# Raw weights in blocks of 512 columns, and operand buffers taken in turn, in a two-layer diffusion backbone

## The chip, the cores and the metric

The kernel runs on one core of one Trainium2 chip, as one program. The metric is the time of one execution in device microseconds; the time before is the median of three runs. Engines are named as in the profile: PE is TensorE's matrix multiplication, PEld its weight load, DVE is VectorE, ACT is ScalarE, POOL is GpSimd, SP is SyncE, which here only issues transfers.

## The reference

Two layers run over 512 latent tokens and 256 context tokens of 1024 features. Layer 0 mixes tokens with windowed attention, layer 1 with a gated linear recurrence in both directions. Each layer ends with a gated feed-forward with a convolution of three tokens. Every sub-layer is preceded by a norm and a shift and scale computed from two conditioning vectors. All is float32. Cut down:

```python
for layer in range(2):
    mod   = silu(c)     @ ada_w[layer] + ada_b[layer]     # 6 x 1024: shift, scale, gate, twice
    mod_c = silu(c_ctx) @ ada_w[layer] + ada_b[layer]
    hx = rms_norm(x, norm1_g) * (1 + sc1) + sh1           # hc the same for ctx
    yx, yc = windowed_gqa(hx, hc, attn_w_in, attn_w_out, ...) if layer == 0 else \
             hgrn2_bidir(hx, hc, hgrn_w_in, hgrn_w_out, ...)
    x = x + g1 * yx
    hx2 = rms_norm(x, norm2_g) * (1 + sc2) + sh2
    gate, val = split(hx2 @ w_up)                         # w_up: 1024 x 2*2816
    x = x + g2 * ((silu(dwconv3(gate)) * val) @ w_down)   # w_down: 2816 x 1024
    # layer 0: ctx goes through the same steps
return x
```

## The kernel before, in words

Activations lie with features on partitions, in 8 groups of 128. Every product of two float32 matrices is done as three TensorE products of a reduced format: each operand is held as a high part and the rest. For a weight, ScalarE copies the raw float32 columns into `wh` and VectorE writes the difference into `wl`; this pair of instructions is called the split here. A pair (`wh`, `wl`) of 512 columns is an operand, and its buffers come from `operand()` (L84), which asks the pools in the list `wsp` one after the other and rotates the list. `ws0` has four buffers of each kind, `wsC`, `wsD` and `wsE`, which are added after the attention, after the first feed-forward and before the second, have two each.

Raw weights land in the pool `wp`: two buffers of 2048 columns (8 KB in each partition). `load_raw` (L90) takes one buffer for all parts of a load, one transfer for each part. Three callers share `wp`:

- `load_w` (L99), for all projections and the second feed-forward's w_up. With `cols` it reads w_down in a transfer of 256 output columns for `nf` feature groups and splits each half through a strided view.
- `load_pair` (L125), for w_up in the first feed-forward, where gate and value are computed by a scheme of seven products for a 2 by 2 block matrix (Strassen's), so sums of the four quarters of the buffer are made on VectorE, partly in place, and seven operands are split from them (L140, L141).
- `ada_steps` (L301), the conditioning: a step loads 128 rows by 2048 columns of `ada_w` in one transfer of 1 MB and multiplies it as it is, in four matmuls side by side in the array's columns (L309). Five groups of eight such steps are strewn over the attention and the first feed-forward; the first group's columns are loaded on their own at the start (`ar`, L296).

The stages are: first norm and projections of keys and values (to about 75 us), attention with the query projections in between (to about 345 us), `attn_out` (L870 on), the first feed-forward (`ffn`, from about 443 us), the recurrence (`hgrn`, from about 1004 us), its output projection `hgrn_out`, and the second feed-forward (from about 1490 us). A feed-forward runs in rounds: some `up(ft)`, each a feature group of gate and value, then for each of four pairs of output groups (`dp`) a load of w_down and the product `dn`, whose result VectorE adds to x (`xl`, `xc`, L1023). `hn` is the scaled x of the next layer, split in the same way (L362, L363); `hs` (L392) holds the sums of the activations that the seven products need, `y` their inputs.

The order of instructions on each engine is made by the framework's scheduler, which simulates the program with its own time model and takes ready instructions by priority; the splits are given a priority of 180 instructions ahead (`W_AHEAD`). A tile's buffer is given on when its last reader is done. All loads of weights go through SP's queue, in the order the scheduler gives them; a load that waits for its buffer holds those behind it.

Of the kernel before, what the change touches and what calls it, by code (L numbers as in the profile page):

```python
# [8 lines left out]
F32 = mybir.dt.float32  # L9
F32R = mybir.dt.float32r  # L10
BF16 = mybir.dt.bfloat16
AF = mybir.ActivationFunctionType
ALU = mybir.AluOpType
# [3 lines left out]
P = 128  # L17
# [14 lines left out]
W_AHEAD = 180  # L32
# [32 lines left out]
def ap(t, off, *dims):  # L65
    return bass.AP(t.tensor, t.offset + off, [list(t.ap[0])] + [list(d) for d in dims])


def f(t):
    return t.bitcast(F32)  # L70


class Kernel:
# [13 lines left out]
        self.wsp = self.wsp[1:] + self.wsp[:1]  # L87
        return pool.tile([P, 512], F32R, tag="wh", name="wh"), pool.tile([P, 512], F32R, tag="wl", name="wl")

    def load_raw(self, parts):  # L90
        raw = self.wp.tile([P, 2048], F32, tag="wr", name="wr")
        n = 0
        for src in parts:
            nk, m = src.shape[1:]
            self.nc.sync.dma_start(out=raw[:, n:n + nk * m].rearrange("p (k m) -> p k m", m=m), in_=src)
            n += nk * m
        return raw, n

    def load_w(self, parts, cols=False):  # L99


        nc = self.nc
        raw, n = self.load_raw(parts)
        nk, m = parts[0].shape[1:]
        out = []
        for lo in range(0, m, P) if cols else range(0, n, 1024):
            size = nk * P if cols else min(1024, n - lo)
            ops = []
            for i in range(0, size, 512):
                c = min(512, size - i)  # L110
                wh, wl = (t[:, 0:c] for t in self.operand())
                src = raw[:, lo + i:lo + i + c]
                with self.tc.high_priority(offset=W_AHEAD):
                    if cols:
                        src = ap(raw[:, i // P * m + lo:i // P * m + lo + 1], 0, (m, c // P), (1, P))
                        wh, wl = (t.rearrange("p (k c) -> p k c", c=P) for t in (wh, wl))
                    nc.scalar.activation(wh, src, AF.Copy)  # L117
                    nc.vector.tensor_tensor(wl, src, f(wh), op=ALU.subtract)  # L118
                    if cols:
                        wh, wl = (t.rearrange("p k c -> p (k c)") for t in (wh, wl))  # L120
                ops.append((wh, wl))
            out.append(ops)
        return out

    def load_pair(self, parts, tmp):  # L125


        nc = self.nc
        raw, n = self.load_raw(parts)
        q = n // 4  # L130
        a11, a12, a21, a22 = (raw[:, i * q:(i + 1) * q] for i in range(4))
        s1 = tmp.tile([P, 512], F32, tag="s1", name="s1")[:, 0:q]
        ops = [tuple(t[:, 0:q] for t in self.operand()) for _ in range(7)]

        def total(o, x, y, op):
            nc.vector.tensor_tensor(o, x, y, op=op)
            return o

        def parts(i, src):
            nc.scalar.activation(ops[i][0], src, AF.Copy)  # L140
            nc.vector.tensor_tensor(ops[i][1], src, f(ops[i][0]), op=ALU.subtract)  # L141


        with self.tc.high_priority(offset=W_AHEAD):
            parts(0, a11)
            parts(1, a12)
            total(s1, a21, a22, ALU.add)
            s3 = total(a21, a11, a21, ALU.subtract)
            s2 = total(a11, s1, a11, ALU.subtract)
            parts(3, s2)  # L150
            parts(6, s3)
            parts(2, s1)
            parts(5, a22)
            s4 = total(a12, a12, s2, ALU.subtract)
            parts(4, s4)
        return ops

    def wcols(self, w, lo, n):
# [142 lines left out]
    def ada_steps(self, l, r, pool, tag, width):  # L301

        nc = self.nc
        ps = pool.tile([P, width], F32, tag=tag, name="ada")
        for k in range(KT):
            raw = self.wp.tile([P, 2048], F32, tag="wr", name="wada")
            nc.sync.dma_start(out=raw, in_=self.a["ada_w"][l, k * P:(k + 1) * P, r * 2048:(r + 1) * 2048])
            for j in range(4):
                nc.tensor.matmul(ps[32 * j:32 * j + 32, 0:512], lhsT=self.cs[:, k, :], rhs=raw[:, j * 512:(j + 1) * 512],  # L309
                                 start=(k == 0), stop=(k == KT - 1), tile_position=(0, 32 * j))  # L310
            if k < KT - 1:
                yield
        sb = self.ap_.tile([P, 512], F32, tag=self.ap_tag, name="adas")
        nc.vector.tensor_copy(sb, ps[:, 0:512])
        yield
        pt = pool.tile([P, width], F32, tag=tag, name="adat")
        for i in range(4):
            nc.tensor.transpose(pt[:, i * P:(i + 1) * P], sb[:, i * P:(i + 1) * P], self.ident)
        m = self.mod[l]
        for v in range(2):  # L320
            o = ap(m[:, v, r * 16:r * 16 + 1], 0, (1, 4), (4, 4))
            b = ap(self.adab[l][:, r * 16:r * 16 + 1], 0, (1, 4), (4, 4))
            i_ = ap(pt[:, v:v + 1], 0, (P, 4), (32, 4))
            nc.vector.tensor_tensor(o, i_, b, op=ALU.add)
        if r == 0:
            self.gain_scale(l, 0, 8, self.n1g[l])
        if r == 2:
            self.gain_scale(l, 1, 32, self.n2g[l])
        yield
# [628 lines left out]
    def ffn(self, l, hs, R, rows, lat_only, tmp, acp, bk, gp, done, side=None):  # L958
        nc, a = self.nc, self.a
        wup, wdn = a["ffn_w_up"][l], a["ffn_w_down"][l]  # L960
        half = C0 // 2 if lat_only else hs[0].shape[3]
        n = LAT if lat_only else TW
# [36 lines left out]
        f0, late, ahead = 0, None, []  # L999
        for r, nf in enumerate(ROUNDS[l]):  # L1000
            gt = ahead + [up(ft) for ft in range(f0 + len(ahead), f0 + nf)]

            ahead = [up(f0 + nf)] if f0 + nf < NFF else []
            if side and r < 5:
                next(side, None)
            for dp in range(KT // 2):
                w = self.load_w([wdn[f0 * P:(f0 + nf) * P, dp * 256:dp * 256 + 256].rearrange("(k p) m -> p k m", p=P)], True)
                outs = [[(bank("dn")[:, 0:m], c) for _, c, m in segs] for _ in range(2)]

                def down(j, ks):  # L1010
                    for _ in self.mm_steps(w[j], ks, lambda k: (gt[k][:, 0], gt[k][:, 1]), outs[j], ks[0] == 0, ks[-1] == nf - 1):
                        pass


                part = dp == 0 and not ahead
                if part:
                    for j in range(2):
                        down(j, range(nf - 1))
                for j in range(2):
                    d = 2 * dp + j  # L1020
                    down(j, (nf - 1,) if part else range(nf))
                    for v, ((o, _), (_, _, x)) in enumerate(zip(outs[j], self.segs(lat_only))):
                        nc.vector.scalar_tensor_tensor(x[:, d], o, self.modc(l, v, 5, d), x[:, d], op0=ALU.mult, op1=ALU.add)  # L1023
                    if f0 + nf == NFF:
                        if late is not None:
                            done(late, bank)
                        late = d
            f0 += nf
# [273 lines left out]
    def run(self, stop=99):  # L1302
        nc, a = self.nc, self.a
        top = ExitStack()
        self.cp = self.pool(top, "const")
        self.wp = self.pool(top, "wp", 2)
        self.ws0 = self.pool(top, "ws0", 4)
        self.wsp = [self.ws0]
        self.setup()
# [6 lines left out]

        xp = self.pool(top, "xp")
        self.xl = xp.tile([P, KT, LAT], F32, tag="xl", name="xl")
        self.wsp.append(self.pool(top, "wsC", 2))
        Rp = self.pool(top, "Rp", 1)  # L1320
        pjs = ExitStack()
        pj = self.pool(pjs, "pj", 2, PSUM)
# [6 lines left out]
        es = ExitStack()  # L1329
        tmp = self.pool(es, "tmpA", 1)  # L1330
# [40 lines left out]
        pjs.close()  # L1371
        pj = self.pool(pjs, "pj", 2, PSUM)
        es = ExitStack()
        self.wsp.append(self.pool(top, "wsD", 2, right=True))
        e2 = ExitStack()
        sc = self.pool(e2, "sc", 2, PSUM)
        lv = self.pool(e2, "lv", 2, PSUM)
# [14 lines left out]
        es = ExitStack()  # L1392
        tmp = self.pool(es, "tmpB", 2)
        acp = self.pool(es, "accB", 1)
        gp = self.pool(es, "gpB", 9)
        self.wsp.append(self.pool(es, "wsE", 2))
        bk = self.pool(es, "bkB", 8, PSUM)
        rows = self.row_factor(acc, True, tmp, bk, "ps", 512, R, -1.0, (gp, "g"))
        ost = {}
# [53 lines left out]
```

## Time and profile before

| | |
|---|---|
| median of 3 runs | 1877.1 us (1875.34 to 1877.72) |
| the profiled execution | 1872.88 us, its span 1871.1 us |
| mean granted TensorE clock | 0.988 |
| HBM read, written | 162.27 MB, 2.10 MB |
| w_up, `wr` | 88 transfers of 512 KB |
| conditioning, `wada` | 40 transfers of 1024 KB |
| hgrn_w_in, `wr` | 40 transfers of 512 KB |
| w_down, `wr` | 16 of 512 KB, 8 of 896 KB, 8 of 384 KB, 4 of 1024 KB |
| attn_w_in, attn_w_out, hgrn_w_out | 6 of 1024 KB, 8 of 512 KB, 8 of 512 KB |

The span is the time from the first to the last recorded work of one execution, and the times of the other views count from its start. "Busy" for PE includes the modelled end of each pipelined matmul, so two matmuls that follow each other overlap in the record. A wait row tells how long an engine stood idle before an instruction and what released it last.

### The profile page before, as it was taken

The numbers are of one execution on the slowest core, as the hardware profiler recorded it, in microseconds if no ns is written. First come the engines' busy times: TensorE is split into PE (matmuls) and PEld (weight loads), VectorE is DVE, ScalarE is ACT, GpSimd is POOL, SyncE is SP. The second block draws the span as 40 slices with busy tenths as digits, with TensorE's granted clock in tenths as the row PEclk, the third lists the DMA queues.
The fourth block names the chain that finished last, engine by engine and source line by source line (L and its number), as shares of the span: only waits on it lengthen the run. The fifth ranks groups of instructions, "written<-read, shape, count | busy, mean of one in ns | idle before, by whom it ended". The sixth has DMA issues, their size and how long they took to land.

```text
span 1871.1 us, 32302 instructions
## 1 busy us (share of the span) xinstructions
PE 1801.3 (96%) x13326; PEld 1576.9 (84%) x13326; DVE 1214.1 (65%) x2243; ACT 754.7 (40%) x1478; POOL 247.4 (13%) x233
## 2 busy tenths in 40 slices
PE   6999999998999999999998999999998999999998
PEld 4976786787888888989887888988886799899997
DVE  5575667466867686766777676777676655455462
ACT  4354555465534252434354333333332443233332
POOL 1233333103201000101013101111110200000000
PEclk9999999998999999999998999999999999999999
DMA  9204104232333333233313212122220332333321
GB/s 309 66 23 158 47 24 169 68 102 68 124 113 102 113 124 113 91 113 124 113 61 90 58 35 58 35 57 58 57 69 24 90 91 91 90 96 96 92 82 65
DMA packets 204416, 166.44 MB, mean 89 GB/s; under 512 B 5149, under 2 KB 198254, under 8 KB 199150
## 3 DMA queue, kind: packets, MB, share of 16 engines
q1 hardware_dynamic: 196608, 160.47, 27.8%
q10 hardware_dynamic: 7662, 3.92, 0.7%
q8 instruction: 105, 1.72, 0.4%
q14 instruction: 41, 0.34, 0.1%
HBM read 162.27 MB, written 2.10 MB: 88 GB/s over the span
## 4 chain that ended last, share of the span: by engine, by line
PE 87%; DVE 5%; DMA 4%; issue 2%; ACT 1%; POOL 1%; SPq 0%; ACTq 0%; POOLq 0%; DVEq 0%
PE dn L170 15%; PE pd L170 13%; PE pZ L188 8%; PE pf L170 8%; PE pV L188 4%; PE pjq L598 4%; PE pv L170 4%; PE ao L170 4%; PE ho L170 3%; PE pq L170 3%; PE pv L824 2%; PE pt L816 2%; PE ada L309 2%; PE pY L188 2%; PE pgate L170 2%; PE kv L598 2%
## 5 line engine op out<-in xcount | busy, mean ns | idle before, releaser
L117 ACT ACTIVATE wh<-wr 128x512 fp32r<-128x512 f32 (+1 forms) x320 | 193.0, 618 | 452.3 <-DMA wr<-in_ffn_w_up 74.8
L118 DVE TENSOR_TENSOR wl<-wr,wh 128x512 fp32r<-128x512 f32 (+1 forms) x320 | 223.6, 705 | 140.3 <-ACT wh L117 138.3
L170 PE MATMUL dn<-g,wh 128*128 128x512 f32 (+1 forms) x1056 | 263.3, 357 | 2.2 <-ACT g L995 2.2
L170 PE MATMUL pd<-hn,wh 128*128 128x256 f32 (+1 forms) x1408 | 227.3, 284 | 0.9 <-issue 0.9
L170 PEld LDWEIGHTS dn<-g,wh 128*128 128x128 f32 x1056 | 175.4, 189 | 32.7 <-ACT g L995 2.8
L170 PEld LDWEIGHTS pd<-hn,wh 128*128 128x128 f32 x1408 | 194.2, 190 | 2.5 <-issue 2.3
L188 PE MATMUL pZ<-hs,wh 128*128 128x386 f32 x704 | 185.2, 345 | 3.0 <-ACT wh L140 1.5
L170 PE MATMUL dn<-g,wl 128*128 128x512 f32 (+1 forms) x528 | 159.4, 356 | 0.0
L140 ACT ACTIVATE wh<-wr 128x512 fp32r<-128x512 f32 x132 | 81.6, 628 | 167.9 <-DMA wr<-in_ffn_w_up 47.4
L170 PE MATMUL pd<-hn,wl 128*128 128x256 f32 x704 | 141.8, 283 | 0.0
L188 PEld LDWEIGHTS pZ<-hs,wh 128*128 128x128 f32 x704 | 128.0, 190 | 15.7 <-ACT wh L140 4.4
L141 DVE TENSOR_TENSOR wl<-wr,wh 128x512 fp32r<-128x512 f32 x132 | 94.0, 717 | 53.6 <-ACT wh L140 53.5
L170 PE MATMUL pf<-hn,wh 128*128 128x512 f32 (+1 forms) x512 | 119.3, 349 | 9.7 <-DVE xc L1023 8.8
L188 PE MATMUL pZ<-hs,wl 128*128 128x386 f32 x352 | 119.4, 343 | 2.2 <-DVE wl L141 2.2
L926 POOL TENSOR_TENSOR gg<-gg,R 128x772 f32<-128x772 f32 x22 | 53.9, 2449 | 458.3 <-DVE gg L925 446.6
L170 PEld LDWEIGHTS pd<-hn,wl 128*128 128x128 f32 x704 | 109.0, 190 | 0.0
L1023 DVE SCALAR_TENSOR_TENSOR xl<-dn,mod,xl 128x512 f32<-128x512 f32 x72 | 53.9, 748 | 73.7 <-PE dn L170 73.6
L170 PEld LDWEIGHTS dn<-g,wl 128*128 128x128 f32 x528 | 87.4, 188 | 14.8
L170 PEld LDWEIGHTS pf<-hn,wh 128*128 128x128 f32 x512 | 80.9, 192 | 22.5 <-ACT wh L117 9.1
L188 PE MATMUL pV<-hs,wh 128*128 128x386 f32 x352 | 92.2, 341 | 5.0 <-ACT hs L392 5.0
L598 PE MATMUL pjq<-wh,hn 128*128 128x256 f32 x384 | 77.8, 291 | 0.0
L188 PEld LDWEIGHTS pZ<-hs,wl 128*128 128x128 f32 x352 | 66.7, 190 | 6.6 <-DVE gg L925 3.4
(299 smaller groups left out, 3807.1 us busy)
## 6 DMA issues: line engine op xcount, KB each, us to landing
wr<-in_ffn_w_up SPq DMA_DIRECT2D x88, 512.0 KB, 5.1
wada<-in_ada_w SPq DMA_DIRECT2D x40, 1024.0 KB, 4.8
wr<-in_hgrn_w_in SPq DMA_DIRECT2D x40, 512.0 KB, 4.2
ar<-in_ada_w SPq DMA_DIRECT2D x32, 256.0 KB, 7.1
wr<-in_ffn_w_down SPq DMA_DIRECT2D x16, 512.0 KB, 4.1
wr<-in_ffn_w_down SPq DMA_DIRECT2D x8, 896.0 KB, 4.7
wr<-in_attn_w_in SPq DMA_DIRECT2D x6, 1024.0 KB, 8.1
wr<-in_attn_w_out SPq DMA_DIRECT2D x8, 512.0 KB, 4.9
```

The costliest lines, as they stand in the source:

```text
L117: nc.scalar.activation(wh, src, AF.Copy)
L118: nc.vector.tensor_tensor(wl, src, f(wh), op=ALU.subtract)
L140: nc.scalar.activation(ops[i][0], src, AF.Copy)
L141: nc.vector.tensor_tensor(ops[i][1], src, f(ops[i][0]), op=ALU.subtract)
L170: nc.tensor.matmul(o, lhsT=wt, rhs=at[:, t0:t0 + o.shape[1]], start=(first and n == 0 and i == 0), stop=(last and n == len(ks) - 1 and i = ...
L188: self.nc.tensor.matmul(ps, lhsT=wt, rhs=at, start=(first and k == 0 and i == 0), stop=(k == nk - 1 and i == 2), skip_group_check=not first)
L309: nc.tensor.matmul(ps[32 * j:32 * j + 32, 0:512], lhsT=self.cs[:, k, :], rhs=raw[:, j * 512:(j + 1) * 512], start=(k == 0), stop=(k == KT ...
L598: nc.tensor.matmul(out, lhsT=x, rhs=y[:, wk], start=(start and k == 0 and j == 0), stop=(stop and k == KT - 1 and j == 2))
L816: nc.tensor.transpose(pt[:, j * P:(j + 1) * P], pr[j][:, b * P:(b + 1) * P], self.ident)
L824: nc.tensor.matmul(pv[a * HD:(a + 1) * HD, 0:256], lhsT=V[:, tl, g, :], rhs=pT[:, a * 256:(a + 1) * 256], start=(b == 0), stop=(b == len(t ...
L926: times = lambda eng, o, x, y: eng.tensor_tensor(o, x, y, op=ALU.mult)
L1023: nc.vector.scalar_tensor_tensor(x[:, d], o, self.modc(l, v, 5, d), x[:, d], op0=ALU.mult, op1=ALU.add)
```

## The change

`wp` becomes eight buffers of 512 columns, the same memory. `block` takes one buffer for each 512 columns of a load and issues one transfer for it; `split` splits one block. `load_w` cuts every part into blocks; w_down is read by 128 output columns at a time, so no strided view is left. `load_pair` loads its four quarters as four blocks. A conditioning step loads four blocks of 512 columns and then does its four matmuls. The list of operand pools is written out anew at each place where it grew: `ws0`, `wsC`, `ws0` during `attn_out` and the first feed-forward, `ws0`, `wsC`, `ws0`, `wsD` in the recurrence, and `wsE` behind these four in the second feed-forward, where each pool stood once in the list before.

```diff
-    def load_raw(self, parts):
-        raw = self.wp.tile([P, 2048], F32, tag="wr", name="wr")
...
+    def block(self, src, pool=None):
+        nk, m = src.shape[1:]
+        raw = (pool or self.wp).tile([P, 512], F32, tag="wr", name="wr")[:, 0:nk * m]
+        self.nc.sync.dma_start(out=raw.rearrange("p (k m) -> p k m", m=m), in_=src)
+        return raw
+
+    def split(self, src, op=None):
+        wh, wl = op or (t[:, 0:src.shape[1]] for t in self.operand())
+        with self.tc.high_priority(offset=W_AHEAD):
+            self.nc.scalar.activation(wh, src, AF.Copy)
+            self.nc.vector.tensor_tensor(wl, src, f(wh), op=ALU.subtract)
+        return wh, wl
+
+    def load_w(self, parts):
+        out = []
         for src in parts:
             nk, m = src.shape[1:]
+            step = 512 // m
+            blocks = [self.block(src[:, k:min(k + step, nk)]) for k in range(0, nk, step)]
+            ops = [self.split(b) for b in blocks]
+            out += [ops[i:i + 2] for i in range(0, len(ops), 2)]
         return out
...
     def load_pair(self, parts, tmp):
-        raw, n = self.load_raw(parts)
-        q = n // 4
-        a11, a12, a21, a22 = (raw[:, i * q:(i + 1) * q] for i in range(4))
+        a11, a12, a21, a22 = (self.block(p[:, i:i + 4]) for p in parts for i in (0, 4))
...
     def ada_steps(self, l, r, pool, tag, width):
         for k in range(KT):
-            raw = self.wp.tile([P, 2048], F32, tag="wr", name="wada")
-            nc.sync.dma_start(out=raw, in_=self.a["ada_w"][l, k * P:(k + 1) * P, r * 2048:(r + 1) * 2048])
+            raw = []
             for j in range(4):
-                nc.tensor.matmul(..., rhs=raw[:, j * 512:(j + 1) * 512], ...)
+                raw.append(self.wp.tile([P, 512], F32, tag="wr", name="wada"))
+                nc.sync.dma_start(out=raw[j], in_=self.a["ada_w"][l, k * P:(k + 1) * P, r * 2048 + j * 512:r * 2048 + j * 512 + 512])
+            for j in range(4):
+                nc.tensor.matmul(..., rhs=raw[j], ...)
...
-                w = self.load_w([wdn[f0 * P:(f0 + nf) * P, dp * 256:dp * 256 + 256].rearrange("(k p) m -> p k m", p=P)], True)
+                w = self.load_w([wdn[f0 * P:(f0 + nf) * P, d * P:d * P + P].rearrange("(k p) m -> p k m", p=P)
+                                 for d in (2 * dp, 2 * dp + 1)])
...
-        self.wp = self.pool(top, "wp", 2)
+        self.wp = self.pool(top, "wp", 8)
...
-        self.wsp.append(self.pool(top, "wsC", 2))
+        wsC = self.pool(top, "wsC", 2)
+        self.wsp = [self.ws0, wsC, self.ws0]
...
-        self.wsp.append(self.pool(top, "wsD", 2, right=True))
+        wsD = self.pool(top, "wsD", 2, right=True)
+        self.wsp = [self.ws0, wsC, self.ws0, wsD]
...
-        self.wsp.append(self.pool(es, "wsE", 2))
+        self.wsp = [self.ws0, wsC, self.ws0, wsD, self.pool(es, "wsE", 2)]
```

More of the change, by code (lines that the diff above doesn't have):

```diff
@@ L88, in operand @@
         return pool.tile([P, 512], F32R, tag="wh", name="wh"), pool.tile([P, 512], F32R, tag="wl", name="wl")
-    def load_raw(self, parts):
-        raw = self.wp.tile([P, 2048], F32, tag="wr", name="wr")
-        n = 0
+    def block(self, src, pool=None):
[9 more added lines that the diff above has]
+        return wh, wl
@@ L93, in load_raw @@
+    def load_w(self, parts):
+        out = []
         for src in parts:
             nk, m = src.shape[1:]
[L95 to L102, printed above, removed]
-        raw, n = self.load_raw(parts)
[L104 to L122, printed above, removed]
@@ L128, in load_pair @@
         nc = self.nc
-        raw, n = self.load_raw(parts)
-        q = n // 4
-        a11, a12, a21, a22 = (raw[:, i * q:(i + 1) * q] for i in range(4))
-        s1 = tmp.tile([P, 512], F32, tag="s1", name="s1")[:, 0:q]
-        ops = [tuple(t[:, 0:q] for t in self.operand()) for _ in range(7)]
+        a11, a12, a21, a22 = (self.block(p[:, i:i + 4]) for p in parts for i in (0, 4))
+        s1 = tmp.tile([P, 512], F32, tag="s1", name="s1")
+        ops = [self.operand() for _ in range(7)]
         def total(o, x, y, op):
@@ L137, in total @@
             return o
-        def parts(i, src):
-            nc.scalar.activation(ops[i][0], src, AF.Copy)
-            nc.vector.tensor_tensor(ops[i][1], src, f(ops[i][0]), op=ALU.subtract)
         with self.tc.high_priority(offset=W_AHEAD):
-            parts(0, a11)
-            parts(1, a12)
+            self.split(a11, ops[0])
+            self.split(a12, ops[1])
             total(s1, a21, a22, ALU.add)
@@ L149, in load_pair @@
             s2 = total(a11, s1, a11, ALU.subtract)
[L150 to L153, printed above, removed]
+            self.split(s2, ops[3])
+            self.split(s3, ops[6])
+            self.split(s1, ops[2])
+            self.split(a22, ops[5])
             s4 = total(a12, a12, s2, ALU.subtract)
-            parts(4, s4)
+            self.split(s4, ops[4])
         return ops
@@ L305, in ada_steps @@
         for k in range(KT):
-            raw = self.wp.tile([P, 2048], F32, tag="wr", name="wada")
-            nc.sync.dma_start(out=raw, in_=self.a["ada_w"][l, k * P:(k + 1) * P, r * 2048:(r + 1) * 2048])
+            raw = []
             for j in range(4):
-                nc.tensor.matmul(ps[32 * j:32 * j + 32, 0:512], lhsT=self.cs[:, k, :], rhs=raw[:, j * 512:(j + 1) * 512],
+                raw.append(self.wp.tile([P, 512], F32, tag="wr", name="wada"))
+                nc.sync.dma_start(out=raw[j], in_=self.a["ada_w"][l, k * P:(k + 1) * P, r * 2048 + j * 512:r * 2048 + j * 512 + 512])
+            for j in range(4):
+                nc.tensor.matmul(ps[32 * j:32 * j + 32, 0:512], lhsT=self.cs[:, k, :], rhs=raw[j],
                                  start=(k == 0), stop=(k == KT - 1), tile_position=(0, 32 * j))
```

## The prediction

> **What bounds the kernel now.** I read the page first: the engines' shares, the busy tenths, the loads.
>
> ```profile
> span 1871.1 us, 32302 instructions
> PE 1801.3 (96%) x13326; PEld 1576.9 (84%) x13326; DVE 1214.1 (65%) x2243; ACT 754.7 (40%) x1478; POOL 247.4 (13%) x233
> DMA  9204104232333333233313212122220332333321
> q1 hardware_dynamic: 196608, 160.47, 27.8%
> ```
>
> TensorE is busy for 1801.3 of 1871.1 us. The DMA engines are near their limit only in the first slice, and q1 takes 27.8% of them over the span. The change touches no matmul and no activation, so what it can win lies in TensorE's 69.8 idle us (1871.1 - 1801.3). The second view is the list of waits, TensorE's own (engine, line, what it waited for: total us, times, longest):
>
> ```profile
> PE ada L275 <- DMA ar<-in_ada_w: 10.8, 3, 9.0
> PE pf L170 <- DVE xc L1023: 8.8, 1, 8.8
> PE pV L188 <- ACT hs L392: 5.0, 1, 5.0
> PE pZ L188 <- DVE wl L141: 2.2, 3, 1.6
> PE dn L170 <- ACT g L995: 2.2, 2, 1.7
> PE ada L309 <- DMA wada<-in_ada_w: 1.9, 2, 1.6
> PE ao L170 <- ACT wh L117: 1.6, 1, 1.6
> PE pZ L188 <- ACT wh L140: 1.5, 4, 0.4
> PE pY L188 <- ACT wh L140: 0.6, 1, 0.6
> ```
>
> The reader is to see how little of it names a weight: wl 2.2, wh 1.5 and 0.6, wh of attn_out 1.6, wada 1.9, together 7.8 us. The big ones are the first loads (10.8), and the borders between stages (8.8 and 5.0). The stages themselves, in the view by stretches (length, then busy us of TensorE, weight load, VectorE, ScalarE, GpSimd, then the granted clock, DMA share, GB/s):
>
> ```profile
> 0.00:40.00 40.00, 22.15 (x224) 15.13 (x228) 24.71 (x76) 18.25 (x31) 5.98 (x9) 1.00 0.91 302
> 400.00:440.00 40.00, 35.73 (x210) 30.67 (x209) 25.56 (x45) 25.11 (x58) 6.56 (x12) 0.98 0.21 63
> 440.00:480.00 40.00, 36.70 (x186) 32.29 (x186) 32.41 (x49) 19.08 (x38) 13.87 (x14) 0.89 0.25 80
> 960.00:1000.00 40.00, 33.20 (x188) 28.92 (x186) 31.86 (x46) 20.14 (x39) 11.79 (x6) 0.98 0.27 80
> 1520.00:1560.00 40.00, 40.00 (x336) 40.00 (x335) 23.92 (x48) 15.07 (x24) 0.00 (x0) 1.00 0.33 91
> ```
>
> The last feed-forward is full (40.00 of 40.00) and has nothing to give. The borders at 400 to 480 and at 960 to 1000 lose 4.3, 3.3 and 6.8 us.
>
> **The change, part by part.** First the loads become more and smaller. The page's DMA issues (KB each, median us to landing) and SP's waits:
>
> ```profile
> wr<-in_ffn_w_up SPq DMA_DIRECT2D x88, 512.0 KB, 5.1
> wada<-in_ada_w SPq DMA_DIRECT2D x40, 1024.0 KB, 4.8
> xs<-in_x ACTq DMA_DIRECT2D x8, 256.0 KB, 2.7
> SPq L95 <- DVE wl L118: 754.3, 69, 34.9
> L307 SPq DMA_DIRECT2D wada<-in_ada_w x40: 327/340/649, 74.1 to 920.5; - x40
> L95 SPq DMA_DIRECT2D wr<-in_ffn_w_up x88: 367/472/1832, 391.7 to 1778.6; - x88
> ```
>
> A pair of w_up goes from two issues to four and a conditioning step from one to four: 88 to 176 and 40 to 160, so 208 more. Each costs SP 0.34 to 0.47 us (the last two rows, min/median/max in ns), so 71 to 98 us over the span. SP sits 754.3 us in one kind of wait alone, for a raw buffer that the split (wl) still reads; the issues hide there. The other loads grow in the same way, by less, and hide in the same wait. Packets of w_down halve from 256 columns to 128; with the DMA engines at a quarter of their time I cost that at nothing. If that cover went, for instance in the first slice, where the share is 0.91, it would cost: the two tiles of attn_w_in between the ar loads become eight loads, six more issues of up to 0.4 us, at most 2.4 us for the ar loads behind them in SP's queue, on which TensorE's 10.8 us hang. Against it ScalarE gets its first block earlier. I take +0.5, ends -1 and +2.4.
>
> Second, a first block lands sooner. The nearest rows are 5.1 us for 512 KB and 2.7 us for 256 KB, on another queue. Where it counts is the entry of the first feed-forward, in the chain of waits (start, us, what):
>
> ```profile
> 427.68 1.10 PE ada L309 x8
> 428.80 4.84 DMA wr<-in_ffn_w_up
> 433.66 0.64 ACT wh L140
> 434.33 0.12 DVE wl L141
> 436.48 0.17 DVE rv L428
> 436.71 0.92 POOL rs L429
> 438.30 2.96 POOL y L376 x2
> 443.30 0.69 PE pV L188
> ```
>
> The load for the second pair starts when the conditioning step at 427.68 frees its tile, lands at 433.64, and ScalarE and VectorE stand still for its split. Behind that split in their queues is the norm's own work (rv, rs, y), for which TensorE waits 5.0 us. With a block of 256 KB the split starts 5.1 - 2.7 = 2.4 us earlier. I take 2 us of it, since y is a chain on GpSimd too; ends 0 (the split is then ordered later anyway) and -5.0 (the wait goes whole). What is late next is y on GpSimd, 2.96 us.
>
> The Trainium skill, SBUF — State Buffer, The DMA setup-cost knee, puts a fixed cost of about 2 us on every transfer and fits 2 us plus bytes over 436 GB/s: by that fit, an estimate, 512 KB take 3.2 us and 256 KB 2.6. The step would then save 0.6 us in place of 2 and the sum would be 1.4 us smaller; its advice to join transfers speaks against this change. The two rows above show a longer 512 KB transfer than the fit, and no row of this case has a 256 KB load of 512-byte runs.
>
> Third, the buffers hold more. A tile of 2048 columns is a slot even where a load has 1024 or less (w_down of four features: 4 x 256 = 1024; the last load of the gate in the recurrence: 1024). As blocks these take 2 of 8. So w_down of four features is fetched for four output pairs ahead, where it was two. With the operands: two buffers of wsC took every second request before, four of ws0 the other half; now ws0 takes two of three. A pair needs seven operands, three or four in wsC's two buffers before, two or three after. Both lift the waits inside the first feed-forward, wl 2.2 + wh 1.5 + wh 0.6 = 4.3 us. I take -3, ends 0 and -4.3. No arithmetic is added: the splits stay the same in number and shape.
>
> Fourth, attn_out and the conditioning in the attention wait 1.6 and 1.9 us for a load. A matmul needs its own block now, not the tile. I take -1.5 of 3.5, ends 0 and -3.5.
>
> Fifth, the end of the first feed-forward. Chain and VectorE's order there:
>
> ```profile
> 966.93 3.21 DMA wr<-in_ffn_w_down
> 970.16 0.64 ACT wh L117
> 972.69 0.85 ACT g L995
> 973.59 2.27 PE dn L170 x11
> 983.36 2.34 DVE L118 TENSOR_TENSOR wl<-wr,wh 128x512 fp32r<-128x512 f32 x1
> 993.11 0.68 DVE L118 TENSOR_TENSOR wl<-wr,wh 128x512 fp32r<-128x512 f32 x1
> ```
>
> A late w_down holds ScalarE; g comes behind it and TensorE waits 1.7 of its 2.2 us there. Deeper loads end this: -1, ends 0 and -2.2. Beside it VectorE splits weights of the next layer between the updates of x on which TensorE's 8.8 us hang; what that may cost is a rival below.
>
> Sum: +0.5 - 2 - 3 - 1.5 - 1 = -7 us. It is made against the profiled execution, 1872.88 us (span 1871.1 and 1.8 around it), which is 4.2 under the median of 1877.1; I carry the difference over: 1877.1 - 7 = 1870 us, 0.37% less. No change that is under 0.2%, 3.75 us, can be told from none.
>
> **The rivals.** *Hidden anyway.* TensorE is full, the order of instructions is made anew for the new loads, and the small waits come back under other names: xc for wl, y for the load. For it: in the stretch from 1520 us no wait is left at all, and the weights' waits are 7.8 us in all. Against it: the chain passes through loads at 428.80 and 966.93 while the DMA engines are three quarters idle. It gives 0 to -3.5, so 1875.
>
> *VectorE is pushed back at the layer's border* (the other side). The splits run with a priority of 180 instructions ahead. If raw blocks of hgrn_w_in are there earlier than now, their splits stand before the updates of x and hn on VectorE, between 975 and 1004 us. A split costs 0.68 us alone and 2.34 beside GpSimd's work (the two rows). Four more of them on the path are 2.7 to 9.4 us; the mean, 6, takes the sum from -7 to -1, so this alone doesn't decide. The point is at 7/1.5, five splits; with eight, a whole set of four parts of two operands, it is +12 - 7 = +5 and 1882 us. Against it: operand buffers limit how many splits can run ahead, six until wsD opens.
>
> *The clock stays up.* The stretch after the border at 440 us has a granted clock of 0.89, and that after 1000 us likewise:
>
> ```profile
> 1000.00:1040.00 40.00, 36.24 (x211) 32.25 (x212) 23.88 (x35) 14.37 (x27) 9.79 (x7) 0.89 0.25 70
> ```
>
> If the wait of 5.0 us there gets too short to lower it, up to 40 x 0.11 = 4.4 us come on top: -11, 1866 us. The Trainium skill, TensorE: Matmul & The Clock Gate, What's actually happening, has the clock halved after an idle window of about 3.4 us; the 5.0 us wait followed by 0.89 agrees.
>
> *No effect of the operand order.* If the waits for wl come from the loads alone, regrouping the operands does nothing, and the third term falls from -3 to some -1.5: 1872, inside the forecast.
>
> **How the numbers follow.** Forecast (1867 to 1873, and the case without operands) 0.42; clock up as well 0.11; hidden anyway 0.30; VectorE pushed back 0.17. Faster by over 0.2%: 0.42 + 0.11 = 0.53; within 0.2%: 0.30; slower: 0.17. The time is that of the likeliest, 1870. The ends: all gains at their bounds are -1 - 5 - 4.3 - 3.5 - 2.2 = -16 and 1861; on the other side I reach to +4, 1881, which leaves out the worst of VectorE's case. As cases of both signs are in that, the likeliest one's own range is 1864 to 1873.
>
> **What the profile after would show.** Right: TensorE's waits for wl, wh and wada under 3 us in sum (7.8 now); w_up with 176 loads of 256 KB landing in under 4 us; TensorE idle near 63 us. The border at 440 us: the wait for hs under 3 us. Wrong: the same idle with other names (hidden anyway); the wait of pf for xc over 12 us with more L118-like splits between 975 and 1004 us (VectorE pushed back); w_up blocks landing after 5 us, which would leave the second term empty; or the first kv matmul later than now, if the loads of the start suffer from the added issues. A new place for TensorE's idle inside the stages that are full now, such as the recurrence, would mean that the order made anew, not any buffer, decided.

## The result, and the profile after

The changed kernel is slower: 1902.0 us (median of 4, 1901.0 to 1903.4) against 1876.8, a ratio of 1.0136 with a 95% interval of 1.0118 to 1.0153. The prediction, 1870 us with 1861 to 1881, has the wrong sign. The profiled execution took 1902.30 us, its span is 1900.3. The head of its page, its loads, and the group of the conditioning's matmuls (from the view of groups by line), first after and then before:

```profile
span 1900.3 us, 33367 instructions
PE 1840.1 (97%) x13326; PEld 1580.7 (83%) x13326; DVE 1228.1 (65%) x2243; ACT 759.8 (40%) x1478; POOL 245.4 (13%) x233
wr<-in_ffn_w_up SPq DMA_DIRECT2D x176, 256.0 KB, 3.0
wada<-in_ada_w SPq DMA_DIRECT2D x160, 256.0 KB, 3.0
L297 PE MATMUL ada<-wada,cs 128*32 128x512 f32 x320 | 84.2, 604 | 1.6 <-DVE xc L883 1.4 <-DMA wada<-in_ada_w 0.2
```

```profile
L309 PE MATMUL ada<-wada,cs 128*32 128x512 f32 x320 | 45.3, 604 | 3.4 <-DMA wada<-in_ada_w 1.9 <-DVE xc L895 1.4
```

TensorE's idle time fell as forecast, from 69.8 to 60.2 us (1900.3 - 1840.1). But it is busy 38.8 us longer with the same 13326 instructions, and one group explains it: the conditioning's matmuls, 45.3 us before and 84.2 after, same count, same mean of 604 ns. Busy time is counted once where instructions overlap, so equal durations with more busy time mean less overlap. The span splits into three parts:

| us | span | TensorE idle | conditioning's matmuls | TensorE's other busy time |
|---|---|---|---|---|
| before | 1871.1 | 69.8 | 45.3 | 1756.0 |
| after | 1900.3 | 60.2 | 84.2 | 1755.9 |

The last column is the same to 0.1 us. So the change is -9.6 of idle time and +38.9 in one group. (The two spans lie 29.2 us apart, the two medians 25.2: the profiled execution of before was quicker than any of its timed runs.) TensorE's order in time shows how. Two stretches of the view, before and then after (start, us, line, tiles, forms, count):

```profile
301.95 1.06 PE L309 MATMUL ada<-wada,cs 128*32 128x512 f32 x8
302.94 0.65 PE L824 MATMUL pv<-pT,V 128*64 128x256 f32 x4
```

```profile
297.93 1.92 PE L297 MATMUL ada<-wada,cs 128*32 128x512 f32 x16
...
301.81 1.04 PE L297 MATMUL ada<-wada,cs 128*32 128x512 f32 x2 [0.17 <-DMA wada<-in_ada_w]
302.79 0.65 PE L812 MATMUL pv<-pT,V 128*64 128x256 f32 x4
303.37 0.66 PE L804 MATMUL pt<-cst,P 128*128 128x128 f32 x4
303.95 1.05 PE L297 MATMUL ada<-wada,cs 128*32 128x512 f32 x2
```

Each of a step's four matmuls is two instructions. All eight, to four column groups of the array, take 1.06 us; one matmul alone, two instructions, takes 1.04. Before, the four depend on one load and become ready together. After, each depends on its own block, the scheduler issues it as soon as it expects the block, and puts attention work between. In TensorE's instruction order the 160 matmuls stand in 41 uninterrupted stretches before and 76 after: 45.3/41 and 84.2/76 are 1.1 us each.

### The profile page after: what moved, and what is told of

Same layout as the page of the kernel before. It is cut to its first block, busy times and chain, and to the rows that moved or that the text cites. A ratio compares the mean times of both kernels' runs of the same rounds, so it can differ in the third digit from the quotient of the medians.

```text
span 1900.3 us, 33367 instructions
## 1 busy us (share of the span) xinstructions
PE 1840.1 (97%) x13326; PEld 1580.7 (83%) x13326; DVE 1228.1 (65%) x2243; ACT 759.8 (40%) x1478; POOL 245.4 (13%) x233
## 4 chain that ended last, share of the span: by engine, by line
PE 92%; DVE 3%; DMA 2%; issue 1%; POOL 1%; ACT 1%; SPq 0%; ACTq 0%; POOLq 0%; DVEq 0%
PE dn L156 15%; PE pd L156 13%; PE pZ L174 10%; PE pf L156 8%; PE pV L174 5%; PE ada L297 4%; PE pjq L586 4%; PE pv L156 4%; PE ao L156 4%; PE pgate L156 3%; PE pq L156 2%; PE pY L174 2%; PE ho L156 2%; PE pv L812 2%; PE pt L804 2%; PE kv L586 2%
## 5 line engine op out<-in xcount | busy, mean ns | idle before, releaser
L101 ACT ACTIVATE wh<-wr 128x512 fp32r<-128x512 f32 (+1 forms) x452 | 279.5, 622 | 662.0 <-PE dn L156 125.2
L102 DVE TENSOR_TENSOR wl<-wr,wh 128x512 fp32r<-128x512 f32 (+1 forms) x452 | 326.4, 726 | 130.2 <-ACT wh L101 119.4
L914 POOL TENSOR_TENSOR gg<-gg,R 128x772 f32<-128x772 f32 x22 | 47.3, 2150 | 475.8 <-DVE gg L913 475.8
L297 PE MATMUL ada<-wada,cs 128*32 128x512 f32 x320 | 84.2, 604 | 1.6 <-DVE xc L883 1.4
L174 PEld LDWEIGHTS pV<-hs,wh 128*128 128x128 f32 x352 | 64.1, 189 | 7.1 <-ACT hs L380 3.2
```

The lines of the kernel that those rows point to most:

```text
L101: self.nc.scalar.activation(wh, src, AF.Copy)
L102: self.nc.vector.tensor_tensor(wl, src, f(wh), op=ALU.subtract)
L174: self.nc.tensor.matmul(ps, lhsT=wt, rhs=at, start=(first and k == 0 and i == 0), stop=(k == nk - 1 and i == 2), skip_group_check=not first)
L914: times = lambda eng, o, x, y: eng.tensor_tensor(o, x, y, op=ALU.mult)
```

## The experiments

Theory 1 is this loss of overlap. Its rivals were the number of small loads, and the new order spoiling other work.

**e1.** The four matmuls kept together, all else as changed.

```diff
-            for j in range(4):
-                nc.tensor.matmul(...j...)
+            last = side(3)                        # side(j): the same matmul
+            with self.tc.issue_after(last.ins):   # behind it in TensorE's order
+                for j in range(3):
+                    side(j)
```

> The changed kernel with one edit: of the four matmuls of a conditioning step the one on the last block is issued first and the other three are queued right behind it on TensorE; loads, blocks and buffers stay as changed. In the order of TensorE's instructions the 160 conditioning matmuls then stand in 43 uninterrupted runs, against 76 in the changed kernel and 41 before. Theory 1 (four matmuls side by side in the array cost about 1.0 us together and 0.97 us each when other work stands between them, so the change lost 35 x 1.0 us there and gained about 9 elsewhere): TensorE busy in these matmuls falls from 84 to about 47 us and the time from 1902 to 1865 to 1871 us. Theory 2 (four times as many small loads are late or hold SP's queue): the loads are untouched, so 1897 to 1905 us. Theory 3 (the order made anew spoiled other work on TensorE): somewhere between, above 1880 us.

Measured: 1877.7 us, ratio to before 1.0006 (0.9996 to 1.0015). The busy time came down to 47.4 us, which is theory 1's number, and so did 24 us of the time, without touching a load. But theory 1's time, 1865 to 1871 us, was missed: the kernel did not become faster than before. The head of its page and the first rows of TensorE's waits say why:

```profile
span 1877.3 us, 33348 instructions
PE 1804.5 (96%) x13326; PEld 1577.8 (84%) x13326; DVE 1232.1 (66%) x2243; ACT 758.6 (40%) x1478; POOL 248.2 (13%) x233
```

```profile
PE ada L261 <- DMA ar<-in_ada_w: 11.4, 3, 9.6
PE ada L297 <- DMA wada<-in_ada_w: 9.2, 10, 2.4
```

The first row, at the start, is nothing new (the kernel before waits 10.8 there). The second is: held back to the last block, the group now waits for it, 9.2 us where the kernel before waits 1.9 and the changed one 0.2. TensorE's idle time is 72.8 us (1877.3 - 1804.5), above the 69.8 of before.

**e2.** The kernel before, only the conditioning's tile filled by four transfers.

```diff
-            nc.sync.dma_start(out=raw, in_=...[..., r * 2048:(r + 1) * 2048])
+            for j in range(4):
+                nc.sync.dma_start(out=raw[:, j * 512:(j + 1) * 512], in_=...[..., 512 columns])
```

> The kernel before with one edit: the conditioning tile of 2048 columns is filled by four transfers of 512 columns in place of one. Tiles, other loads and operands stay as before. The 160 matmuls stand in 73 uninterrupted runs (41 before). Theory 1: 32 more runs of about 1 us, so TensorE busy in them goes from 45 to about 78 us and the time from 1877 to 1903 to 1911 us, slower than the whole change, since this has none of its gains. Theory 2 (the number of small loads as such): 120 of the 342 added transfers, a third of the loss, so 1882 to 1888 us. Theory 3: not above 1880 us.

Measured: 1917.9 us, ratio 1.0214 (1.0197 to 1.0232). More than expected: the busy time of the group is 82.4 us (+37.1, for 32 more stretches), and the waits for wada are 7.9 us, which the expectation had left out. This one edit costs more than the whole change.

**e3 and e4.** The operand lists: e1 with the old lists, and the kernel before with the new ones.

> The kernel of e1 (changed kernel, conditioning matmuls kept together) with the operand pools listed as before, each pool once. 41 runs of conditioning matmuls. Tells how much of the gain is the operand order. If the split's waits came from operand buffers: 2 to 4 us slower than e1, 1869 to 1875 us. If they came from the loads alone: within 1.5 us of e1.

> The kernel before with the operand pools listed as in the change and nothing else. Loads as before, 44 runs of conditioning matmuls. Theory 1: 3 more runs are +3 us and the operands give back 1 to 3, so 1874 to 1880 us. Theory 3 (a new order alone costs much): more than 1885 us.

Measured: e3 1881.7 us, ratio 1.0027 (1.0015 to 1.0038), 4 us over e1, the top of what was expected if the operand buffers matter. e4 1861.7 us, ratio 0.9920 (0.9906 to 0.9935): the expectation is missed by 12 us on the good side. TensorE's waits for split weights, in e3 and in e1:

```profile
PE pZ L174 <- DVE wl L102: 8.0, 4, 2.8
```

```profile
PE pZ L174 <- ACT wh L101: 1.8, 3, 0.6
PE pZ L174 <- DVE wl L102: 1.7, 2, 1.2
```

With the old lists the seven products wait for a split, with the new they wait less; in e4 no row of a wait for wl or wh is left. The operand order is a gain: 15 us by the medians in the kernel before, 4 us with the blocks, where e1's larger wait for wada (9.2 us for e3's 6.7) takes some of it back.

**e5.** e4 with the four matmuls kept together at raised priority, one load of 1 MB for each step.

```diff
+            with self.tc.issue_after(last.ins), self.tc.high_priority(offset=400):
```

> e4 (the kernel before with the new operand lists, one load of 1 MB for each conditioning step) with the four matmuls of each step kept together: the last is issued first, the other three right behind it at a raised priority. 38 runs in TensorE's order (e4: 44). Theory 1 (each uninterrupted run costs about 1.0 us whether it holds two, four or eight of these instructions): TensorE busy in them falls from 48.4 to about 40 us, and the time from 1861.7 to 1852 to 1857 us. If the grouping costs a wait for the load instead: TensorE's wait for wada over 3 us and 1860 us or more.

Measured: 1857.4 us, ratio 0.9915 (0.9900 to 0.9931). The group's busy time is 42.2 us in 38 stretches, TensorE's wait for wada 0.2. The time is at the slow end of the 1852 to 1857 expected. No version has a lower ratio, but e4's 0.9920 lies within its interval, so no gain in time over e4 is shown.

**e6.** e5 with four transfers for each step. The order on TensorE, ScalarE and VectorE is e5's.

> e5 with the conditioning tile filled by four transfers of 256 KB in place of one of 1 MB. The order of instructions on TensorE, ScalarE and VectorE is the same as in e5, so only the transfers differ. Theory A (four transfers of 256 KB are done later than one of 1 MB, because SP issues each at 0.34 us and the tile's last quarter counts): TensorE waits 6 to 10 us longer for wada, as in e1 (9.2 us), and the time is 6 to 10 us over e5. Theory B (what e1 lost against e4 lies in the block buffers, not in the transfers): within 2 us of e5.

Measured: 1865.7 us, ratio 0.9955 (0.9938 to 0.9971), 8 us over e5 by the medians. So theory A: TensorE waits 6.1 us for wada, 5.9 more than in e5. The largest of these waits lies in the attention, where six steps follow each other. SP's and TensorE's order in time there, e5 and then e6:

```profile
160.04 17.90 SPq L307 DMA_DIRECT2D wada<-in_ada_w  x6
...
164.83 1.06 PE L309 MATMUL ada<-wada,cs 128*32 128x512 f32 x8
168.92 1.07 PE L309 MATMUL ada<-wada,cs 128*32 128x512 f32 x8
...
180.14 1.06 PE L309 MATMUL ada<-wada,cs 128*32 128x512 f32 x8
```

```profile
161.79 24.26 SPq L308 DMA_DIRECT2D wada<-in_ada_w  x24
...
168.86 1.23 PE L310 MATMUL ada<-wada,cs 128*32 128x512 f32 x8 [2.37 <-DMA wada<-in_ada_w]
174.45 1.07 PE L310 MATMUL ada<-wada,cs 128*32 128x512 f32 x8
...
185.68 1.06 PE L310 MATMUL ada<-wada,cs 128*32 128x512 f32 x8
```

The first step's matmuls start 4.8 us after the first issue in e5 and wait for nothing; in e6 they start 7.1 us after it, and TensorE stands still for 2.37. The later steps keep the same pace in both: from the second to the fifth it is 11.2 us (168.92 to 180.14, 174.45 to 185.68). So in this burst the four quarters cost at its head, where the matmuls wait for the load; behind it they are hidden. Behind the wait the granted clock is lower too, 0.91 in the 20 us from 160 us for e5's 1.00, which can be part of the rest of the 8 us. The Trainium skill, SBUF — State Buffer, The DMA setup-cost knee, which puts a fixed cost on each transfer and advises large ones, agrees in sign. Whether it is the cost of each transfer, the shorter runs of 2 KB in place of 8, or the spacing of SP's four issues was not separated.

**e7.** The price of the overlap by itself: the kernel before with the four matmuls in one column group in seven of eight steps.

```diff
+                g = 32 * j if k == 0 else 0
-                nc.tensor.matmul(ps[32 * j:32 * j + 32, 0:512], ..., tile_position=(0, 32 * j))
+                nc.tensor.matmul(ps[g:g + 32, 0:512], ..., tile_position=(0, g))
```

> The kernel before, but in steps 2 to 8 of each group of eight all four matmuls go to the first of the four column groups and add up there, so they cannot run side by side (the conditioning vectors are not those of the reference; loads, counts and sizes are as before). Measures the price by itself: 35 of 40 steps with four matmuls in series. Theory 1 with 0.97 us for each matmul: 35 x 3 x 0.97 = 102 us more, 1979 us, TensorE busy in these matmuls from 45 to about 147 us. If side by side bought nothing: 1877 us.

Measured: 1957.7 us, ratio 1.045 (1.0422 to 1.0479). The busy time is 132.2 us, so 86.9 us for 105 matmuls that lost their company: 0.83 us each, somewhat under the 0.97 expected. In e7's trace a step in series has a record of 3.62 us, less than four times the 1.04 of one alone: in the record each begins before the modelled end of the one ahead.

**e8.** A dose between: the kernel before with two transfers for each step.

> The kernel before with the conditioning tile filled by two transfers of 1024 columns. 59 uninterrupted runs of conditioning matmuls, between before (41) and e2 (73). Theory 1: 18 x 1.0 us for the runs and the waits for wada halfway to e2's 7.9 us, +3: 1894 to 1901 us, TensorE busy in them about 64 us. Theory 2 (number of loads): 40 added ones, a third of e2's 120, so +14 us, 1891 us, with the busy time of these matmuls unchanged at 45 us.

Measured: 1896.1 us, ratio 1.0119 (1.0101 to 1.0136), and the group's busy time is 66.2 us where theory 2 has 45. Its time lies in theory 1's range too (1894 to 1901; theory 2 had 1891). Over all runs with the four groups in use the busy time goes with the uninterrupted stretches and not with the loads:

| | transfers per step | stretches | busy us |
|---|---|---|---|
| e5 | 1 | 38 | 42.2 |
| e12 | 1 | 38 | 42.2 |
| e6 | 4 | 38 | 42.4 |
| e9 | 4 | 39 | 43.6 |
| e11 | 1 | 40 | 42.6 |
| before | 1 | 41 | 45.3 |
| e3 | 4 | 41 | 46.2 |
| e1 | 4 | 43 | 47.4 |
| e4 | 1 | 44 | 48.4 |
| e8 | 2 | 59 | 66.2 |
| e2 | 4 | 73 | 82.4 |
| after | 4 | 76 | 84.2 |

**e9 and e11.** Are blocks for the weights good or bad? e9 is the changed kernel with e5's grouping; e11 is e9 with one tile of 2048 columns for the conditioning and four blocks for the weights.

```diff
-        self.wp = self.pool(top, "wp", 8)
+        self.wp = self.pool(top, "wp", 4)
+        self.wa = self.pool(top, "wa", 1)         # conditioning: one tile, one load
```

> The changed kernel whole (blocks everywhere, new operand lists), with the four conditioning matmuls kept together as in e5: 39 runs in TensorE's order (e1: 43). Theory 1: TensorE busy in them 42 to 43 us as in e5, 5 less than e1's 47.4, so 1870 to 1874 us. What then still lies between this and e6 (1865.7, same four loads and operands, but weights in tiles of 2048 columns) is the price of the block buffers: 5 to 8 us. If blocks cost nothing beside the loads of the conditioning: within 2 us of e6.

> e9 with the raw memory divided in another way: one tile of 2048 columns for the conditioning, filled by one load of 1 MB, and four blocks of 512 columns for the weights (the same 16 KB). 40 runs of conditioning matmuls. If e9's remainder comes from the four loads of a step: TensorE's wait for wada falls from about 9 us to under 3 and the time to 1861 to 1867 us. If the depth of the raw buffers matters (four blocks in place of eight, one conditioning tile): new waits for wh, wl or wada and 1872 us or more.

Measured: e9 1875.8 us, ratio 1.0002 (0.9990 to 1.0014); e11 1859.3, ratio 0.9916 (0.9901 to 0.9932), as e5. TensorE's wait for the conditioning's loads, e9 and then e11:

```profile
PE ada L297 <- DMA wada<-in_ada_w: 11.1, 9, 2.5
```

```profile
PE ada L295 <- DMA wada<-in_ada_w: 1.5, 2, 0.8
```

e9 lies 2 us above its expected 1870 to 1874. Its expectation that what is left to e6 is the price of the block buffers does not hold for the weights: with blocks for the weights and a whole tile for the conditioning e11 loses nothing against e5, even with half as many blocks. Of the 17.9 us between the spans of e9 and e11, 9.6 are the waits shown and 1.0 is the matmuls' busy time (43.6 and 42.6). The rest is spread over other idle time and TensorE's other busy time (1755.6 and 1751.1) and was not traced to a place. e11 changes two things for the conditioning, the size of the load and a buffer of its own, and no run parts them. e6, with the same four transfers into whole tiles, has 6.1 us of these waits for e9's 11.1, so some of e9's price may come from sharing eight blocks with the weights.

**e12.** The term of an earlier first block: e5 with each load of weights in transfers of 512 columns into the same tile.

```diff
-            self.nc.sync.dma_start(out=raw[:, n:n + nk * m]..., in_=src)
+            for k in range(0, nk, step):          # step = 512 // m
+                c = min(step, nk - k)
+                self.nc.sync.dma_start(out=raw[:, n:n + c * m]..., in_=src[:, k:k + c])
+                n += c * m
```

> e5 (two raw tiles of 2048 columns, conditioning in one load and kept together, new operand lists) with each load of weights cut into transfers of 512 columns into the same tile. Tells what an earlier first block is worth with nothing else changed, the second term of the prediction (-2 us at the entry of the first feed-forward). Theory of the prediction: -1 to -3 us against e5, 1854 to 1856 us, and the wait of pV for hs (4.4 us in e5) under 3 us. If it is hidden: within 1.5 us of e5's 1857.4 and the wait unchanged. If small loads land late, as those of the conditioning did: +3 us or more.

Measured: 1861.5 us, ratio 0.9922 (0.9905 to 0.9939), against e5's 0.9915: no gain, and no loss clear of noise. (The ratios are compared, as the two had different medians of before, 1875.4 and 1874.1.) Two rows of e12's waits:

```profile
PE ada L312 <- DMA wada<-in_ada_w: 4.6, 3, 2.2
PE pV L191 <- ACT hs L400: 2.2, 1, 2.2
```

The wait for hs at the entry of the feed-forward is halved, 2.2 us for e5's 4.4 in all, as the term said. At the same time the wait for the conditioning's load rose to 4.6 us from 0.2. But e11, whose w_up comes in the same 256 KB and lands in 2.9 us, waits 4.9 us for hs. So small loads alone do not set this wait.

## Why the prediction was wrong

The step that failed stands at the start of the prediction: "The change touches no matmul and no activation, so what it can win lies in TensorE's 69.8 idle us". It was meant as a bound on the gain, and I took it for a bound on the loss too. The busy time was treated as fixed, though that of one group depends on what stands next to it: the conditioning's matmuls ran side by side because one load released all four. The fourth part names that very release ("A matmul needs its own block now, not the tile") and books it as -1.5 us. The wait did go, from 1.9 to 0.2 us; the 38.9 us were not in the sum. The profile of before had the sign of it: 320 instructions of 604 ns are 193 us, and the group is busy for 45.3 (in e7, where most stand in series, it is 191 against 132.2). No rival held this either. *VectorE is pushed back* was the one for a slower kernel, and it did not happen: TensorE's wait of pf for xc is 8.7 us after and 8.8 before. All four signs of being right came true: waits for wl, wh and wada of 0.2 us in sum, 176 loads of w_up that land in 3.0 us, 60.2 us of idle time, 2.2 us for hs. None of them looked at busy time.

The other terms, against the profile after:

```profile
PE pf L156 <- DVE xc L1012: 8.7, 1, 8.7
PE pZ L174 <- DVE hs L381: 2.3, 1, 2.3
PE pV L174 <- ACT hs L380: 2.2, 1, 2.2
```

```profile
0.00:40.00 40.00, 22.42 (x213) 14.84 (x213) 24.17 (x73) 18.46 (x31) 5.88 (x9) 1.00 0.92 301
400.00:440.00 40.00, 39.76 (x236) 34.90 (x234) 23.88 (x41) 21.50 (x47) 0.50 (x5) 1.00 0.20 60
440.00:480.00 40.00, 33.27 (x162) 26.84 (x163) 30.12 (x50) 22.48 (x51) 16.43 (x21) 0.91 0.32 93
```

- Idle time in sum: -9.6 us, where the terms gave -7 and "near 63" was 60.2. The number fits, but in part by luck: the matmuls did not wait for the late blocks because they had parted. With the group kept whole and all else as changed, e1 is idle for 72.8 us and e9 for 75.8, more than before, and neither is faster (ratios 1.0006 and 1.0002). So the fourth part's -1.5 had its wait right only at the price of the 38.9 us.
- The start (+0.5): 17.6 us of idle time in the first 40, 17.9 before. The six added issues cost nothing that shows.
- The entry of the first feed-forward (-2): the wait of pV for hs is 2.2 us for 5.0, but 2.3 came as a wait of pZ for hs, and the stretches from 400 to 480 us lose 7.0 us for 7.6. The loads do land sooner (3.0 us for 5.1), but little of it reached TensorE, and e12 and e11 disagree on what it does to the wait.
- Buffers and operands (-3): the waits for wl and wh of the first feed-forward, 4.3 us, are gone. The size was too small: the operand lists alone are worth 15 us by e4's median. By the profiles it is 11.3 us of span: 8.6 less idle time, 5.8 less other busy time (1756.0 to 1750.2) and 3.1 more in the conditioning's matmuls. The mean clock was 0.991 for 0.988 in these two executions, so how much of the 5.8 is the operands' is not shown. The variant of *no effect of the operand order* is refuted.
- The clock: 0.91 for 0.89 in the stretch at 440 us and 1.00 for 0.98 in the one ahead of it, so of the 4.4 us of *the clock stays up* at most 1.6 came (80 x 0.02); the stretches also no longer hold quite the same work.
- The late w_down (-1): the wait of dn for g is gone from the list.

In all: the operand lists gain, blocks for the weights give nothing either way beside them (e11 against e5), and the conditioning's load in four costs, through the matmuls' overlap if they are free to part, and through late quarters if they are not.

## What to carry to other kernels

Before a load or a buffer is cut, look at what its single arrival releases together: instructions that share the array at once are grouped by that one release, and a scheduler that fills gaps can part them. Compare a group's count times its mean with its busy time in the profile: where the product is several times larger, the order of these instructions is worth money and should be pinned, or the load kept whole. Test the parts of a combined change alone: here one part was worth 0.8% and was buried under another. And when a prediction counts idle time alone, say why busy time should stay as it is.

## What the runs showed of the hardware that was not expected

Four float32 matmuls of 32 output rows and 512 columns, each in its own column group, cost 1.06 us together and one alone 1.04. The Trainium skill, TensorE: Matmul & The Clock Gate, Measured speedup vs the span model, gives such a pack the time of one matmul and some 4 ns for each further tile; the traces agree, and e7 shows the other side, 0.83 us for each that loses its company. The same 1 MB was there for the matmuls within 4.8 us of its issue as one load, and 7.1 us after the first issue as four (e5 and e6, the first step of the burst), though one quarter alone lands sooner (3.7 us median against 4.8, e6 and e5):

```profile
wada<-in_ada_w SPq DMA_DIRECT2D x40, 1024.0 KB, 4.8
```

```profile
wada<-in_ada_w SPq DMA_DIRECT2D x160, 256.0 KB, 3.7
```
